# Layer hand-over in a two-layer hybrid backbone: left-over products in two turns, value products between two half norms, early products four pairs at a time, context keys in the weight ring

## Chip, cores and metric

One core of one Trainium2 chip runs the whole program. The metric is device microseconds of one execution, as the median of several. Engines are named as the profile names them: PE (matmul) and PEld (its weight load), DVE, ACT, POOL, and SP, which issues most DMAs. All matmuls here are in the fp32r format, and each logical product is three of them: high by high, high by low and low by high part.

## What is computed

Two layers over 1024 latent tokens of width 1024, with a context of 256 tokens. Layer 0 mixes tokens by retention and by softmax attention, layer 1 by a gated MLP. Each layer ends in a squared-ReLU channel MLP. What bears on the change:

```python
# layer 0, attention: latent queries read context keys and latent keys
s = jnp.einsum('bqkgd,bskd->bkgqs', qi, k) * scale       # k = [context keys 256 | latent keys 1024]
p = jax.nn.softmax(s, axis=-1)
# every layer
x = x + g1 * o_lat
x = x + g2 * (jnp.square(jax.nn.relu(modulate(rms_norm(x, norm2_g), sh2, sc2) @ w1)) @ w2)
# layer 1, mixer
h = modulate(rms_norm(x, norm1_g), sh1, sc1)
z = jax.nn.gelu(h @ w_in); u, v = z[..., :1024], z[..., 1024:]
```

## The kernel before

The stream is held feature-major: eight tiles of 128 features by 1024 tokens, treated as two halves of 512 tokens. A value is split into a high part (an ACT copy that rounds) and a low part (a DVE subtraction); `split` does this (lines 79 to 81). Weights come through a ring of four staging tiles (`st_tile`) and are split into a ring of twelve tiles (`w_tile`, lines 69 to 72). From the end of the attention on, all PSUM tiles come from one pool of eight banks.

**Attention (lines 577 to 654).** `att_load` loads the latent keys `akl` and queries into the weight ring, and the context keys `akc` and values `av` into the pool `ap_`, which opens at line 571 in the place of the pools `hp` and `tabs` (closed at lines 563 and 564). `tabs` holds the cosine and sine tables that `rope` reads (lines 388 to 390). `scores` makes a 128x256 product with `akc` (`s2`) and two 128x512 products with `akl` (`s1`), takes the maximum of both, and writes the exponentials to `pr`; `mx`, `sm` and `pr` are in `ap_` as well.

**Channel MLP.** Both its matrices are multiplied by a scheme of seven block products in place of eight (names A11, A12, S1 to S4, A22 against B11, B21, T1 to T4, B22). Up: sixteen pairs `p` of hidden blocks. For the first eight (`NPRO`), `up_first` (line 847) makes the two products that need the first token half only, A11 by B11 and A12 by B21, two pairs at a time: two B11 blocks, whose results ACT copies to `ef` and SP stores to `e_d`, then two B21 blocks on top in the same bank, squared by ACT into `sf` and stored to `s_d`. Each block is twelve matmuls. After each block `tick()` takes one step of `norm_forms` (line 745) of the second half: the norm's sum (`nsum`), its broadcast (`nbc`) with the first quarter of the forms, then one quarter each; a quarter takes two buffers `t1`, `t2` of the pool tag `t`, which has four buffers and also serves `ef` and `sf`. `mlp_up` (line 782) then takes p = 0 to 15 in order: for p below 8 (`early`) it reads `e_d` and `s_d` back and makes five products, else seven.

Down: `job` (line 884) multiplies a band of hidden blocks; after each product DVE adds the bank to the stream (`stt`, line 882). The last two jobs are called with `keep=True`: the products S1 by T1 (`todo[7]`) and S4 by B22 (`todo[8]`) of output tiles 1 to 3 are handed back as closures, the left-overs. They reach the second token half only. `todo[8]` also holds `done(q, 1)`, which adds the squares of the finished tiles to the norm's sum (`norm_acc`) and stores them with a POOL DMA.

**Hand-over from layer 0 to layer 1 (lines 975 to 1029).** For the first half: `norm_rstd` (four small matmuls `nsum`, DVE, a power on POOL), `norm_bc` (four small matmuls `nbc`), then for each of eight tiles DVE writes `hp`, ACT the high part of `hm` and DVE its low part. Then all left-overs. Then the same norm for the second half. Then the value products `pv` of layer 1: for each of two column groups, eight token tiles `tt` (0 to 3 first half, 4 to 7 second half), each eight steps `k` of three matmuls; the first four tiles of group 0 go step by step side by side. ACT applies GELU to each finished tile (`v_out`).

The order in the program text is not always the order on an engine: within the limits of the data each engine has its own order, which the profile shows.

Of the kernel before, what the change touches and what calls it, by code (L numbers as in the profile page):

```python
# [10 lines left out]
F32 = mybir.dt.float32  # L11
F32R = mybir.dt.float32r
# [4 lines left out]
P = 128  # L17
# [15 lines left out]
def hybrid_retention_gqa_chunkmlp_kernel(tc, I, out):  # L33
# [543 lines left out]
    def att_load(G, hh):  # L577
        if hh == 0:
            akl = load_w(ak_d[G, :, TC:], f"ak{G}")
            akc = ap_.tile([P, 2, TC], F32R, tag="akc", bufs=2, name=f"akc{G}")  # L580
            av = ap_.tile([P, 2, 10 * P], F32R, tag="av", bufs=2, name=f"av{G}")
            avd = av_d[G].rearrange("p n d -> p (n d)")
            for dst, src in ((akc, ak_d[G, :, 0:TC]), (av[:, :, 0:1024], avd[:, 0:1024]), (av[:, :, 1024:], avd[:, 1024:])):
                st = st_tile()[:, :src.shape[-1]]
                nc.sync.dma_start(st, src)
                split(st, dst[:, 0], dst[:, 1])
            kv_t[G] = (akl, akc, av)
        aq_t[2 * G + hh] = load_w(aq_d[2 * G + hh], f"aq{2 * G + hh}")
# [193 lines left out]
    def mlp_up(l, F, s_d, utemp, pro):  # L782
        def src(p):
            return lambda i: [I["w1"][l, p, i]]

        for p in range(16):
            f = w_forms(src(p), f"u{l}_{p}", skip=p in pro)
            a, b, e = (mm_tile([P, H], f"u{n}{l}_{p}") for n in "abe")

# [56 lines left out]

    def up_first(l, F, s_d, e_d):

        for p0 in range(0, NPRO, 2):
            ps = [mm_tile([P, H], f"uf{l}_{p0 + d}") for d in range(2)]  # L850
            W = []
            for d in range(2):
                R = w_raw(I["w1"][l, p0 + d, 0])
                W.append([w_form(R[:, j], f"wf{l}_{p0 + d}_{j}") for j in range(2)])
            for d in range(2):
                block(ps[d], W[d][0], F["B11"], True)
                tick()
                e1 = tmp(f"ef{l}_{p0 + d}")
                nc.scalar.copy(e1, ps[d])
                nc.sync.dma_start(e_d[p0 + d], e1)  # L860
            for d in range(2):
                block(ps[d], W[d][1], F["B21"], False)
                tick()
                s11 = tmp(f"sf{l}_{p0 + d}")
                nc.scalar.activation(s11, ps[d], AF.Relu)
                nc.scalar.activation(s11, s11, AF.Square)
                nc.sync.dma_start(s_d[p0 + d][0], s11)

    def mlp_down(l, xt, s_d, done):
# [14 lines left out]
        def job(*parts, keep=False):  # L884
# [35 lines left out]
            for i in range(7):  # L920
                for go in todo[i]:
                    go()
            return todo[7] + todo[8]

        job((1, 0, 1), (2, 0, 2))
        job((3, 0, 3))
        for i in range(13):
            job((i % 4, i, i + 4))
        left = job((1, 13, 16), keep=True)
        return left + job((2, 14, 16), (3, 15, 16), keep=True)  # L930

    def layer_mlp(l, F, close_xt, s_d, e_d, x1_d, done):
        up_first(l, F, s_d, e_d)
# [40 lines left out]

    close_xd, xt, left = layer_mlp(0, F, close_xa, s_d, e_d, x1_d, done0)
    hm = [[None] * KT for _ in range(2)]
    for hf in range(2):
        if hf:
            for g in left:
                g()  # L980
        rs = norm_rstd(nt, ss1[hf], H)
        pb = norm_bc(rs, H)
        gs, sh = mods[(1, 1)], mods[(1, 0)]
        for k in range(KT):
            hp = tmp("hp")
            hm[hf][k] = o = f_tile(f"hm_{hf}_{k}")
            nc.vector.scalar_tensor_tensor(hp, xt[k][:, hf * H:(hf + 1) * H], gs[:, k:k + 1], pb, ALU.mult, ALU.mult)
            nc.scalar.activation(o[:, 0, :], hp, AF.Identity, bias=sh[:, k:k + 1])
            nc.vector.scalar_tensor_tensor(o[:, 1, :], hp, sh[:, k:k + 1], o[:, 0, :].bitcast(F32),
                                           ALU.add, ALU.subtract)  # L990
    close_xd()


# [3 lines left out]
    nc.sync.dma_start(wsT, I["wsT"])  # L997
    bsb = gp.tile([P, 8, P], F32, name="bsb")
    nc.sync.dma_start(bsb, I["bs"].partition_broadcast(P))
    zg = [f_tile(f"zg{g}", F32).rearrange("p a (b c) -> p (a b) c", c=P) for g in range(8)]  # L1000
    vs = gp.tile([P, 8, NTT], F32, name="vs")
    for cg in range(2):
        W = [load_w(I["wv"][cg, 2 * j:2 * j + 2].rearrange("k p n -> p k n"), f"wv{cg}_{j}") for j in range(4)]
        pvs = {}

        def v_mm(tt, k):
            hf, o = tt // 4, (tt % 4) * P
            if k == 0:
                pvs[tt] = mm_tile([P, H], f"pv{cg}_{tt}")
            wc = slice((k % 2) * H, (k % 2) * H + H)  # L1010
            mm3(pvs[tt], hm[hf][k][:, 0, o:o + P], hm[hf][k][:, 1, o:o + P],
                W[k // 2][0][:, wc], W[k // 2][1][:, wc], k == 0, k == KT - 1)

        def v_out(tt):
            for j in range(4):
                nc.scalar.activation(zg[cg * 4 + j][:, tt, :], pvs[tt][:, j * P:(j + 1) * P], AF.Gelu_apprx_tanh)

        for t0 in (0, 4):
            if cg + t0 == 0:
                for k in range(KT):  # L1020
                    for tt in range(4):
                        v_mm(tt, k)
                for tt in range(4):
                    v_out(tt)
                continue
            for tt in range(t0, t0 + 4):
                for k in range(KT):
                    v_mm(tt, k)
                v_out(tt)
        for j in range(4):  # L1030
            g = cg * 4 + j
            for q in range(2):
# [59 lines left out]
        close_za()  # L1092

    close_xd, xt, left = layer_mlp(1, F, close_xb, s_d, e_d, x1_d, done1)
    for g in left:
        g()
    close_xd()
    close_f()
# [69 lines left out]
```

## Time and profile before

| | us |
|---|---|
| median of 3 runs (lowest, highest) | 2358.17 (2357.75, 2369.09) |
| the profiled execution, whole | 2363.36 |
| its span, first to last instruction | 2361.60 |
| PE busy in the span | 2244.6 (95%) |
| DVE busy | 1645.0 (70%) |
| ACT busy | 1026.2 (43%) |
| POOL busy | 143.3 (6%) |
| mean granted TensorE clock | 0.982 of full |

Busy time is the time in which an engine has at least one instruction under way. A row of the timeline gives the start, the length, the engine, the line of the kernel, the operation with its written and read tiles and shapes, and in brackets how long the engine stood idle before it and what released it. A line can be that of a helper (75 to 77 are the three matmuls of a product, 80 and 81 the two halves of a split), so tiles say more than lines.

### The profile page before, as it was taken

Reading aid. Unit: us, or ns where it says so; the run is one execution under the profiler, and the core shown is the slowest. Engines: PE = TensorE matmul, PEld = TensorE weight load, DVE = VectorE, ACT = ScalarE, POOL = GpSimd, SP = SyncE. Lnnn points to the kernel's source line nnn. Section 1 sums busy time; section 2 is a strip of 40 time slices with the busy share of each in tenths; the row PEclk is TensorE's granted clock in tenths of the full one; section 3 lists DMA queues with packets and bytes.
Section 4 is the critical chain, followed back from the end, with each engine's and each line's share of the span. In section 5 each row is a group of like instructions: output and inputs, shape, how many; then the busy total and the mean of one; then the engine's idle time right before and its main releaser. Section 6 shows DMA issues by size and latency. Waiting matters only on the chain.

```text
span 2361.6 us, 28820 instructions
## 1 busy us (share of the span) xinstructions
PE 2244.6 (95%) x10412; PEld 1807.9 (77%) x10412; DVE 1645.0 (70%) x2706; ACT 1026.2 (43%) x1809; POOL 143.3 (6%) x133
## 2 busy tenths in 40 slices
PE   6998999989999999999999969999999999999999
PEld 1887787769887788877777848888878888777777
DVE  5656679699857786568877673444678755788885
ACT  3511112277736545564444333323465555544441
POOL 2323221000000000000000010000000000000000
PEclk9999999999999999999999979999999999999999
DMA  8244556440153764466445341114447544754442
GB/s 296 74 138 155 159 176 194 138 137 19 36 201 110 232 214 162 147 212 211 150 143 144 98 142 54 45 45 170 138 143 245 170 147 147 276 161 143 147 138 81
DMA packets 158688, 350.71 MB, mean 149 GB/s; under 512 B 16593, under 2 KB 30417, under 8 KB 158545
## 3 DMA queue, kind: packets, MB, share of 16 engines
q1 hardware_dynamic: 154960, 336.28, 44.1%
q0 software_dynamic: 3584, 12.58, 1.4%
q8 instruction: 82, 1.34, 0.2%
q14 instruction: 62, 0.50, 0.1%
HBM read 262.29 MB, written 86.51 MB: 148 GB/s over the span
## 4 chain that ended last, share of the span: by engine, by line
PE 79%; DVE 8%; DMA 6%; issue 3%; ACT 3%; POOL 1%; SPq 0%; DVEq 0%; ACTq 0%; POOLq 0%
PE dbd L75 4%; PE ub L75 4%; PE ub L77 4%; PE ub L76 4%; PE dbd L76 4%; PE dbd L77 4%; PE po L76 3%; PE po L77 3%; PE po L75 2%; PE ue L75 2%; PE ue L76 2%; PE ue L77 2%; PE ded L75 2%; PE pl L77 2%; PE ded L76 2%
## 5 line engine op out<-in xcount | busy, mean ns | idle before, releaser
L80 ACT CAST wr<-st 128x512 fp32r<-128x512 f32 (+2 forms) x404 | 277.8, 693 | 481.9 <-PE dbd L76 90.1
L81 DVE TENSOR_TENSOR wr<-st,wr 128x512 fp32r<-128x512 f32 (+2 forms) x400 | 308.6, 777 | 176.1 <-ACT wr L80 158.0
L75 PE MATMUL dbd<-sT,wr 128*128 128x512 f32 x384 | 155.0, 405 | 13.7 <-DVE xd L882 9.4
L75 PE MATMUL ub<-T,wr 128*128 128x512 f32 x384 | 153.1, 399 | 11.6 <-DVE ur L822 6.8
L75 PE MATMUL pl<-wr,h 128*128 128x512 f32 x384 | 154.5, 402 | 0.2 <-ACT zrl L484 0.2
L76 PE MATMUL dbd<-sT,wr 128*128 128x512 f32 x384 | 153.2, 399 | 0.0
L77 PE MATMUL dbd<-sT,wr 128*128 128x512 f32 x384 | 153.0, 399 | 0.0
L77 PE MATMUL ub<-T,wr 128*128 128x512 f32 x384 | 152.6, 397 | 0.0
L76 PE MATMUL ub<-T,wr 128*128 128x512 f32 x384 | 152.6, 397 | 0.0
L76 PE MATMUL pl<-wr,h 128*128 128x512 f32 x384 | 152.5, 397 | 0.0
L77 PE MATMUL pl<-wr,h 128*128 128x512 f32 x384 | 152.5, 397 | 0.0
L882 DVE SCALAR_TENSOR_TENSOR xd<-dbd,mcol,xd 128x512 f32<-128x512 f32 x152 | 112.9, 747 | 45.7 <-PE dbd L77 45.7
L80 ACT CAST sT<-sT 128x512 fp32r<-128x512 f32 x128 | 79.2, 620 | 83.9 <-DMA sT<-s_d 79.4
L139 DVE SCALAR_TENSOR_TENSOR macc<-st,scc,macc 128x1024 f32<-128x1024 f32 x70 | 92.4, 1321 | 24.2 <-DMA st<-in_mod_w 23.7
L75 PEld LDWEIGHTS dbd<-sT,wr 128*128 128x128 f32 x384 | 73.1, 190 | 39.4 <-DVE xd L882 16.6
L81 DVE TENSOR_TENSOR sT<-sT 128x512 fp32r<-128x512 f32 x128 | 87.3, 686 | 19.0 <-ACT sT L80 18.8
L75 PEld LDWEIGHTS ub<-T,wr 128*128 128x128 f32 x384 | 72.6, 189 | 30.6 <-DVE ur L822 7.7
L81 DVE TENSOR_TENSOR sB<-sB 128x512 fp32r<-128x512 f32 x96 | 66.0, 688 | 33.0 <-ACT sB L80 33.0
L791 ACT ACTIVATE ur<-ur 128x512 f32<-128x512 f32 x96 | 60.8, 633 | 60.6 <-DVE ur L837 22.9
L77 PEld LDWEIGHTS dbd<-sT,wr 128*128 128x128 f32 x384 | 73.0, 190 | 17.7
L80 ACT CAST sB<-sB 128x512 fp32r<-128x512 f32 x96 | 59.5, 620 | 61.4 <-DMA sB<-s_d 59.3
L77 PEld LDWEIGHTS ub<-T,wr 128*128 128x128 f32 x384 | 72.6, 189 | 17.5
(363 smaller groups left out, 5854.0 us busy)
## 6 DMA issues: line engine op xcount, KB each, us to landing
st<-in_w SPq DMA_DIRECT2D x132, 512.0 KB, 4.4
s_d<-ur SPq DMA_DIRECT2D x208, 256.0 KB, 2.3
st<-in_mod_w SPq DMA_DIRECT2D x80, 512.0 KB, 4.4
sT<-s_d SPq DMA_DIRECT2D x128, 256.0 KB, 2.9
sB<-s_d SPq DMA_DIRECT2D x96, 256.0 KB, 3.2
st<-in_wo SPq DMA_DIRECT2D x32, 512.0 KB, 3.6
st<-in_wg SPq DMA_DIRECT2D x24, 512.0 KB, 5.1
mw<-in_mod_w SPq DMA_DIRECT2D x16, 512.0 KB, 6.4
```

The lines of the kernel that those rows point to most:

```text
L75: nc.tensor.matmul(ps, lhsT=a_hi, rhs=b_hi, start=first, stop=False, skip_group_check=more)
L76: nc.tensor.matmul(ps, lhsT=a_hi, rhs=b_lo, start=False, stop=False, skip_group_check=more)
L77: nc.tensor.matmul(ps, lhsT=a_lo, rhs=b_hi, start=False, stop=last, skip_group_check=more)
L80: nc.scalar.copy(hi, src)
L81: eng.tensor_tensor(lo, src, hi.bitcast(F32), ALU.subtract)
L139: nc.vector.scalar_tensor_tensor(acc, st, scc[:, k, 0:1], acc, ALU.mult, ALU.add)
L791: nc.scalar.activation(t, t, AF.Relu)
L882: nc.vector.scalar_tensor_tensor(o, ps_, g, o, ALU.mult, ALU.add)
```

## The change

Four edits. The context keys take a tile of the weight ring in place of one of the pool `ap_`. `up_first` works on four pairs at a time, and `mlp_up` takes pair 8, which needs all seven products, ahead of pairs 0 to 7. The two last down jobs hand their left-overs back as two lists, all S1 by T1 products and all S4 by B22 products. At the hand-over the order becomes: first list, norm and forms of the first half, second list, the value weights of column group 0 and its products for the first token half, norm and forms of the second half, the GELUs of the first four tiles, then the remaining value products.

```diff
     def att_load(G, hh):
         if hh == 0:
             akl = load_w(ak_d[G, :, TC:], f"ak{G}")
-            akc = ap_.tile([P, 2, TC], F32R, tag="akc", bufs=2, name=f"akc{G}")
+            akc = w_tile()[:, :2 * TC].rearrange("p (a b) -> p a b", a=2)
...
-        for p in range(16):
+        for p in [NPRO] + list(range(NPRO)) + list(range(NPRO + 1, 16)):
             f = w_forms(src(p), f"u{l}_{p}", skip=p in pro)
...
-        for p0 in range(0, NPRO, 2):
-            ps = [mm_tile([P, H], f"uf{l}_{p0 + d}") for d in range(2)]
+        for p0 in range(0, NPRO, 4):
+            ps = [mm_tile([P, H], f"uf{l}_{p0 + d}") for d in range(4)]
             W = []
-            for d in range(2):
+            for d in range(4):
                 R = w_raw(I["w1"][l, p0 + d, 0])
                 W.append([w_form(R[:, j], f"wf{l}_{p0 + d}_{j}") for j in range(2)])
-            for d in range(2):
+            for d in range(4):
                 block(ps[d], W[d][0], F["B11"], True)
                 tick()
...
-            for d in range(2):
+            for d in range(4):
                 block(ps[d], W[d][1], F["B21"], False)
                 tick()
...
-            return todo[7] + todo[8]
+            return todo[7], todo[8]
...
-        left = job((1, 13, 16), keep=True)
-        return left + job((2, 14, 16), (3, 15, 16), keep=True)
+        la, lb = zip(job((1, 13, 16), keep=True), job((2, 14, 16), (3, 15, 16), keep=True))
+        return la[0] + la[1], lb[0] + lb[1]
...
-    for hf in range(2):
-        if hf:
-            for g in left:
-                g()
+
+    def norm_rows(hf):
         rs = norm_rstd(nt, ss1[hf], H)
         pb = norm_bc(rs, H)
...
+    def v_weights(cg):
+        for j in range(4):
+            zg[cg * 4 + j] = f_tile(f"zg{cg}{j}", F32).rearrange("p a (b c) -> p (a b) c", c=P)
+        return [load_w(I["wv"][cg, 2 * j:2 * j + 2].rearrange("k p n -> p k n"), f"wv{cg}_{j}") for j in range(4)]
...
+    for g in left[0]:
+        g()
+    norm_rows(0)
+    for g in left[1]:
+        g()
+    wv0 = v_weights(0)
+    for k in range(KT):
+        for tt in range(4):
+            v_mm(0, wv0, tt, k)
+    norm_rows(1)
+    for tt in range(4):
+        v_out(0, tt)
     close_xd()
...
     for cg in range(2):
-        W = [load_w(I["wv"][cg, 2 * j:2 * j + 2].rearrange("k p n -> p k n"), f"wv{cg}_{j}") for j in range(4)]
...
+        W = v_weights(1) if cg else wv0
+        for tt in range(0 if cg else 4, NTT):
+            for k in range(KT):
+                v_mm(cg, W, tt, k)
+            v_out(cg, tt)
...
-    for g in left:
+    for g in left[0] + left[1]:
         g()
```

## Rows read from the trace of the kernel before

**Rows 1.** Page, engines: busy us (share of span) and number of instructions.

```profile
PE 2244.6 (95%) x10412; PEld 1807.9 (77%) x10412; DVE 1645.0 (70%) x2706; ACT 1026.2 (43%) x1809; POOL 143.3 (6%) x133
```

**Rows 2.** Waits of PE, whole run: who waits for whom, total us, times, longest.

```profile
PE nsum L195 <- DVE ss L189: 10.5, 2, 5.3
...
PE ded L75 <- DVE xd L882: 8.2, 8, 4.9
...
PE s L75 <- ACT akc L80: 6.3, 1, 6.3
PE uf L75 <- ACT ef L859: 6.0, 6, 1.2
...
PE ub L75 <- ACT wr L80: 4.8, 2, 2.4
...
PE nbc L205 <- POOL rs L199: 3.9, 3, 1.4
```

**Rows 3.** Timeline of PE at the hand-over: start, length, instruction, idle before it.

```profile
1372.73 0.80 PE L75 MATMUL dbd<-sT,wr 128*128 128x512 f32 x1 [4.06 <-ACT wr L80]
...
1381.54 0.40 PE L77 MATMUL dbd<-sT,wr 128*128 128x512 f32 x1
1387.26 1.87 PE L195 MATMUL nsum<-ones,ss 128*128 128x1 f32 x8 [5.32 <-DVE ss L189]
1390.56 2.08 PE L205 MATMUL nbc<-ident,rs 128*128 128x128 f32 x8 [1.44 <-POOL rs L199]
...
1402.73 0.79 PE L75 MATMUL ded<-sB,w_d 128*128 128x512 f32 x1 [4.92 <-DVE xd L882]
...
1419.97 0.77 PE L75 MATMUL pv<-wr,hm 128*128 128x512 f32 x1
...
1443.00 0.39 PE L75 MATMUL pv<-wr,hm 128*128 128x512 f32 x1
```

**Rows 4.** Timeline of DVE at the hand-over.

```profile
1385.72 1.48 DVE L189 TENSOR_TENSOR ss<-ss,sq 128x512 f32<-128x512 f32 x2
...
1392.68 2.06 DVE L987 SCALAR_TENSOR_TENSOR hp<-xd,mcol,nbc 128x512 f32<-128x512 f32 x3 [3.28 <-PE nbc L205]
1394.66 2.07 DVE L989 SCALAR_TENSOR_TENSOR hm<-hp,mcol,hm 128x512 fp32r<-128x512 f32 x3
```

**Rows 5.** Busy time by stretch: us, PE, PEld, DVE, ACT, POOL, clock, DMA share, GB/s.

```profile
786.00:1056.00 270.00, 266.53 (x1143) 214.47 (x1142) 188.27 (x304) 143.93 (x243) 2.38 (x4) 1.00 0.56 187
1382.00:1420.00 38.00, 19.73 (x69) 16.39 (x69) 24.19 (x37) 10.85 (x18) 6.46 (x10) 0.67 0.28 97
```

**Rows 6.** Timeline of PE in the up stage of layer 0.

```profile
735.15 1.05 PE L195 MATMUL nsum<-ones,ss 128*128 128x1 f32 x8
...
738.94 1.06 PE L205 MATMUL nbc<-ident,rs 128*128 128x128 f32 x8
...
770.09 0.50 PE L75 MATMUL uf<-B,wr 128*128 128x512 f32 x1 [1.16 <-ACT ef L859]
777.12 0.50 PE L75 MATMUL uf<-B,wr 128*128 128x512 f32 x1 [1.16 <-ACT ef L859]
785.35 0.50 PE L75 MATMUL ub<-T,wr 128*128 128x512 f32 x1 [2.38 <-ACT wr L80]
```

**Rows 7.** Instructions on tile uf, 732 to 763 us: ns, first and last start.

```profile
L75 PE MATMUL uf<-B,wr x40: 393/394/482, 732.3 to 761.5; 128*128 128x512 f32 x40
...
L865 ACT ACTIVATE sf<-uf x2: 578/584/591, 747.6 to 755.7; 128x512 f32<-128x512 f32 x2
```

**Rows 8.** Timeline of ACT at the start of the attention.

```profile
478.82 0.41 ACT L80 CAST akc<-st 128x256 fp32r<-128x256 f32 x1 [6.67 <-DVE ropeb L390]
...
482.78 1.28 ACT L606 ACT_TABLE_LOAD   x1
```

**Rows 9.** Timeline of PE at the start of the attention, third query tile.

```profile
485.78 0.50 PE L75 MATMUL s<-wr,wr 128*128 128x512 f32 x1 [2.56 <-ACT pr L607]
```

**Rows 10.** Timeline of ACT, GELUs of the first four token tiles.

```profile
1441.14 2.85 ACT L1016 ACTIVATE zg<-pv 128x128 f32<-128x128 f32 x16 [9.38 <-PE pv L77]
```

More of the change, by code (lines that the diff above doesn't have):

```diff
@@ L990, in hybrid_retention_gqa_chunkmlp_kernel, with v_mm, v_out @@
                                            ALU.add, ALU.subtract)
+    zg = [None] * 8
+    pvs = {}
+    def v_weights(cg):
+        for j in range(4):
+            zg[cg * 4 + j] = f_tile(f"zg{cg}{j}", F32).rearrange("p a (b c) -> p (a b) c", c=P)
+        return [load_w(I["wv"][cg, 2 * j:2 * j + 2].rearrange("k p n -> p k n"), f"wv{cg}_{j}") for j in range(4)]
+    def v_mm(cg, W, tt, k):
+        hf, o = tt // 4, (tt % 4) * P
+        if k == 0:
+            pvs[tt] = mm_tile([P, H], f"pv{cg}_{tt}")
+        wc = slice((k % 2) * H, (k % 2) * H + H)
+        mm3(pvs[tt], hm[hf][k][:, 0, o:o + P], hm[hf][k][:, 1, o:o + P],
+            W[k // 2][0][:, wc], W[k // 2][1][:, wc], k == 0, k == KT - 1)
+    def v_out(cg, tt):
+        for j in range(4):
+            nc.scalar.activation(zg[cg * 4 + j][:, tt, :], pvs[tt][:, j * P:(j + 1) * P], AF.Gelu_apprx_tanh)
+    for g in left[0]:
[10 more added lines that the diff above has]
+        v_out(0, tt)
     close_xd()
@@ L999, in hybrid_retention_gqa_chunkmlp_kernel @@
     nc.sync.dma_start(bsb, I["bs"].partition_broadcast(P))
-    zg = [f_tile(f"zg{g}", F32).rearrange("p a (b c) -> p (a b) c", c=P) for g in range(8)]
     vs = gp.tile([P, 8, NTT], F32, name="vs")
     for cg in range(2):
-        W = [load_w(I["wv"][cg, 2 * j:2 * j + 2].rearrange("k p n -> p k n"), f"wv{cg}_{j}") for j in range(4)]
[L1004 to L1029, printed above, removed]
+        W = v_weights(1) if cg else wv0
[3 more added lines that the diff above has]
+            v_out(cg, tt)
         for j in range(4):
```

## Prediction

> **What bounds the kernel now.** I read the page first: PE is busy for 95% of the span [rows 1], so an edit earns time only where PE stands still. The next view is therefore the table of PE's waits over the whole run [rows 2]. Four kinds of wait in it stand at places that the change touches: the sum of a norm that waits for DVE (10.5 us in two waits), a left-over product `ded` that waits for DVE (8.2), the early products `uf` that wait for ACT's copies `ef` and the first late product `ub` that waits for a weight form (6.0 and 4.8, over two layers), and the first score that waits for the context keys (6.3). The third view, PE's timeline at each of these places, tells what stood ready meanwhile.
>
> At the **hand-over** the last main product of the down stage starts at 1381.54; then PE waits 5.32 us for the sum `ss`, 1.44 us between the norm's sum and its broadcast, and 4.92 us ahead of the second turn of left-overs. The wait for the second sum is the other half of the 10.5 us. The value products start at 1419.97 and those of the second token half at 1443.00 [rows 2, 3]. From 1382 to 1420 PE's clock is granted at 0.67 on average, so the matmuls between the waits run at the lower level (1.2 GHz) for part of the time, and DVE works for 24.19 of the 38 us [rows 5]. So this stretch is a chain of short steps on three engines, with 36 left-over matmuls and 96 value matmuls that lie behind steps they don't depend on.
>
> **Part 1, the hand-over.** The edit moves the first turn of left-overs (18 matmuls) ahead of norm 0, the second turn (18) and the 96 value matmuls of the first token half ahead of norm 1. Nothing is added or removed; every DMA is the same, and the POOL stores of the second turn still precede the power of norm 1. I rebuild the chain:
>
> - A matmul of 512 columns costs 0.245 us at the full clock: 24 of them lie between the starts 770.09 and 777.12, of which 1.16 us is a wait [rows 6]. So a turn of 18 takes 4.4 us. The first runs from about 1381.9 to 1386.3, beside the sums.
> - The sum `ss` of the first half is done at 1387.2, since its two last additions start at 1385.72 and take 1.48 [rows 4]. Nothing in it depends on the left-overs. What could delay it are the three bank additions of the first turn on DVE, which take about the 0.7 us each of the additions beside them: 0 to 2 us; I take 0, because the matmuls that release them end only shortly before the sum.
> - Norm 0: `nsum` 1.05, wait for the power 1.44, `nbc` 1.06 (durations of the same steps when PE was busy before [rows 3, 6]): broadcast done at 1390.8. The first low part of `hm` is done 2.8 us after the end of the broadcast (1392.64 to about 1395.4 [rows 3, 4]): 1393.6.
> - The second turn takes 4.4 us from 1390.8, so PE is the later one, and the value products start at 1395.2 in place of 1419.97. Their forms keep ahead: DVE makes one eighth with two operations of 0.66 us (three in 2.06 [rows 4]), 1.3 us, and PE needs twelve matmuls for it, 2.9 us. The bank additions and squares of the second turn lie beside them.
> - The first half's value products take 23.0 us (1419.97 to 1443.00 [rows 3]): end at 1418.2.
> - The cover is now gone from norm 1: in the kernel before its forms ran beside these 23 us. After the change PE pays `nsum` 1.05, 1.44, `nbc` 1.06 and 2.8 to the first form, 6.35 us. So the second half starts at 1424.6 in place of 1443.00: a gain of 18.4.
> - Behind that, the second half's forms come at 1.3 us per step. If PE goes through one token tile after the other, its first tile ends with the last form, 16 operations of 0.66 or 10.6 us after the broadcast, and 0.7 for the last three matmuls, against 2.8 and 24 matmuls (5.5) without starving: 3.0 us lost. If it fills in the other tiles, nothing is lost. ACT may also put the table load and the 16 GELUs (1.28 and 2.85 [rows 8, 10]) ahead of the forms: up to 4.1 us. The text of the kernel puts the forms first, so I take 1 us for both together.
>
> Part 1 gives 17.4 us. Its bounds are 9.3 (18.4, less 2.0 for bank additions ahead of the sum, 3.0 and 4.1) and 20.0 (the second turn wholly in the power's wait, so that the start is set by the first form at 1393.6).
>
> One rule speaks against this part. The row of the table load shows 1.28 us [rows 8]. By the Trainium skill ("ScalarE: Activation LUTs", What ACT_TABLE_LOAD costs) each switch to another set of functions also costs a drain, 2.66 us in all; then a load ahead of norm 1's forms would cost 1.4 us more, and the sum would be 16.0 in the bad order and unchanged in the good one.
>
> **Part 2, early products and pair 8.** Per layer PE waits about 3 us for `ef` (three waits, two of 1.16) and 2.38 for the first S2 form [rows 2, 6]. The copies are late because of their buffers and their place on ACT, not because of the products: by 763 us PE had done 120 `uf` matmuls, ten blocks, but ACT had squared only two [rows 7]. So the eight B11 blocks were finished, and the B21 blocks stood behind copies that ACT makes after the squares of the pair before. With four pairs in a group, four copies come ahead of four squares, and a B21 block follows its B11 block by three blocks, 8.8 us, in place of one. Pair 8 then gives PE 24 matmuls, 5.9 us, that need only B11 and B21 forms, over a wait of 2.38. All is moved, nothing added; SP's stores and read-backs are the same. The whole of 6.0 + 4.8 = 10.8 us is the upper bound. The lower is 0 or below: four copies hold all four buffers of tag `t` that the second half's `t1` and `t2` need, so a norm step can wait for a store. I take 10.0, since those forms are done long before PE needs them, and a step that comes some us late is covered.
>
> **Part 3, context keys.** PE waits 6.30 us for them, but ACT's copy of them waited for the last reader of the rotary tables [rows 2, 8]. That is the release of the space under the pool `ap_`, and the softmax's own buffers `mx` and `pr` are in the same pool. So the two small score products move forward, but the exponentials stay behind the same release; they also need a table load of 1.28 us, and the third query tile waits for them until 485.78 [rows 8, 9]. What goes is DVE's and ACT's split of the keys and the wait of the maximum for the late product: I take 1 us, with 0 and 2.5 as bounds (2.5 is the wait of the third tile [rows 9]). The keys' two tiles shift the weight ring, so that one output weight less can be made ready before the attention ends; the same 2.5 bounds what that could cost, and I take nothing.
>
> **Sum.** 17.4 + 10.0 + 1.0 = 28.4 us. Against the profiled execution, 2363.36 us (span 2361.60), that is 2335.0; the median of the runs shown is 5.2 us lower, 2358.17, and gives 2329.8.
>
> **Rivals.**
> - *Starved second half.* The wait moves from ahead of the value products to their middle: 3.0 and 4.1 us of Part 1 are paid, 11.3 + 10 + 1 = 22.3, 2336. For it: the forms come at 1.3 us a step and PE's text order is by tile. Against it: the second half's forms stand ahead of the GELUs.
> - *Up stage gains nothing.* The four buffers of tag `t` are the limit, and with four pairs they are held longer: 18.4, 2339.8.
> - *The order on PE stays.* The value products and left-overs were ready during the waits of 5.3 us and PE didn't take them, so the engine's order isn't free: if norm 1 still comes first, the change doesn't do what it says, and only 11 us remain, 2347.
> - *More goes than I count.* The wait of 4.06 us ahead of the last down job [rows 3] goes too, as that job's forms are placed anew: 20.0 + 4.1 + 10.8 + 2.5 = 37.4, 2320.8.
> - *Slower.* Pair 8 first puts seven weight forms in a ring of twelve ahead of the early pairs' five. If each following pair then finds its S2 form late, as the first pair does now, the wait of 2.38 us is paid per pair. It decides from twelve pairs of the 32 on (28.4 / 2.38); with the 16 pairs of one layer it is 38 us, 2368. Against it: from 786 to 1056 PE is busy for 266.5 of 270 us and DVE for 188 [rows 5], so forms are made with room to spare.
>
> **How the numbers follow.** Chances: forecast 0.39, starved second half 0.20, up stage gains nothing 0.12, order stays 0.12, more goes 0.12, slower 0.05. The forecast and three cases on its side hold 0.83, from 2321 to 2340 us; with 9.3 of Part 1 and 3 of Part 2 (one layer's wait for the first form) on the one side, 12.3 us, and the fourth rival with 5 us for other reordering on the other, the range is 2316 to 2346. Half a per cent, 11.8 us, is about what a measurement can tell from no change. Faster by more: 0.83; within: 0.12 (order stays); slower: 0.05.
>
> **What would show it.** PE's timeline after the change: `ded` ahead of the first `nsum`; `pv` from about 1395, less what was gained before it; one wait of 1.4 and one of about 2.8 us around the second `nbc`, in the middle of the value products, and no 5 us wait; no wait of `uf` for `ef` and none of `ub` for a form near 785; a first wait of scores for the keys gone and a wait for `pr` at nearly the same time as before. I am wrong if `pv` still starts behind two norms, if the waits for `ef` stay, or if the waits between `nbc` and the second half of `pv` sum to over 15 us.

## The result and the profile after

| | before | after |
|---|---|---|
| median of the runs beside one another, us | 2358.45 (2357.75 to 2369.09) | 2330.31 (2326.75 to 2337.72) |
| ratio to the kernel before, 95% interval | | 0.9878 (0.9859 to 0.9898) |
| profiled execution, us (span) | 2363.36 (2361.6) | 2337.72 (2335.9) |

The kernel became 1.2% faster: 28.1 us by the medians, 25.6 by the two profiled executions. By stages, in us; the last two columns are means over all kernels of this study in which the stage is as before or as after, with their lowest and highest trace:

| stage | trace before | trace after | all as before | all as after |
|---|---|---|---|---|
| attention: first score to output projection | 170.5 | 171.2 | 170.7 (170.5 to 170.7, six) | 171.1 (170.7 to 171.4, four) |
| up stage, layer 0: first `uf` to first `dbd` | 325.7 | 324.0 | 328.5 (325.7 to 330.4, five) | 323.1 (322.0 to 324.0, four) |
| down stage of layer 0 and value products: first `dbd` to last `pv` | 450.7 | 431.3 | 446.9 (442.6 to 450.7, four) | 429.8 (427.7 to 431.3, five) |
| up stage, layer 1 | 328.2 | 321.8 | 327.5 (326.5 to 328.2, five) | 322.1 (320.8 to 323.5, four) |
| down stage, layer 1 (unchanged) | 325.6 | 324.8 | 323.7 (320.3 to 327.6, all) | |

By the means the hand-over gave 17.1 us, the two up stages 5.4 each, and the attention lost 0.4: 27.5 us of the 28.1. A stage with the same instructions differs by several us from trace to trace, so that a single pair of traces gives 19.4, 1.7 and 6.3 for the same three; the means are the better measure. (One of the five traces behind the 429.8 is that of the kernel without the value weights' low parts, whose hand-over isn't quite that of after.) A narrower stretch spreads less: the last 60 main down products (`dbd` and `dad`), the left-overs, the two norms and the value products, the same 512 matmuls in every kernel. From the first start to the last it takes 149.7 us on the mean of the four kernels with the old hand-over (147.8 to 151.5) and 131.9 on the mean of five with the new one (131.7 to 132.3). By this measure the hand-over gave 17.8 us. PE's idle time in it falls from 23.6 us to 11.1, on the means; for the rest fewer of its matmuls, those of the norms among them, run at the lower clock.

The page and PE's waits over the whole run, as in [rows 1, 2] (who waits for whom: total us, times, longest):

```profile
PE 2243.3 (96%) x10412; PEld 1811.7 (78%) x10412; DVE 1645.4 (70%) x2706; ACT 1023.4 (44%) x1809; POOL 143.3 (6%) x133
```

```profile
PE ub L75 <- DVE ur L822: 8.3, 2, 4.7
PE tal L444 <- ACT av L80: 6.2, 1, 6.2
PE dbd L75 <- DVE xd L882: 6.1, 8, 1.6
...
PE ded L75 <- DVE xd L882: 5.6, 7, 1.5
...
PE nbc L205 <- POOL rs L199: 4.8, 3, 2.3
PE pv L75 <- ACT hm L986: 3.2, 2, 1.6
PE s L75 <- ACT pr L607: 3.1, 2, 2.6
...
PE nsum L195 <- DVE ss L189: 2.7, 1, 2.7
```

PE's busy time over the same instructions is 1.3 us less; the rest of the gain is idle time. Of the four kinds in [rows 2] at places that the change touches, the two for `ef` and for the first S2 form are gone, that for the sum `ss` fell from 10.5 us to 2.7, that of `ded` from 8.2 to 5.6. The wait for the keys has a successor of the same length: `tal`, a transpose, for ACT's copy of the context values.

PE at the hand-over, as in [rows 3] (start, length, instruction, idle before it):

```profile
1363.86 0.39 PE L75 MATMUL ded<-sT,w_d 128*128 128x512 f32 x1
...
1369.54 0.47 PE L75 MATMUL ded<-sB,w_d 128*128 128x512 f32 x1 [1.37 <-DVE xd L882]
...
1385.28 1.05 PE L195 MATMUL nsum<-ones,ss 128*128 128x1 f32 x8 [2.67 <-DVE ss L189]
1388.67 2.08 PE L205 MATMUL nbc<-ident,rs 128*128 128x128 f32 x8 [2.35 <-POOL rs L199]
1392.35 0.79 PE L75 MATMUL pv<-wr,hm 128*128 128x512 f32 x1 [1.59 <-ACT hm L986]
...
1416.44 0.95 PE L195 MATMUL nsum<-ones,ss 128*128 128x1 f32 x8
1418.80 1.16 PE L205 MATMUL nbc<-ident,rs 128*128 128x128 f32 x8 [1.41 <-POOL rs L199]
1421.55 0.80 PE L75 MATMUL pv<-wr,hm 128*128 128x512 f32 x1 [1.59 <-ACT hm L986]
```

Left-over products `ded` now start at 1363.86, among the products of the last down job, and both turns end ahead of the first `nsum`. The job's two waits in the kernel before, of 4.06 us [rows 3] and of 1.71 (at 1366.31), have shrunk to one of 1.37. Behind the job stands one chain (sum, power, broadcast, first high part) and then the value products of the first half, 27.6 us earlier than in [rows 3]; the chain of norm 1 stands in their middle.

Busy time of the same stretch, as in [rows 5], and of two short ones behind waits (us, PE, PEld, DVE, ACT, POOL, clock, DMA share, GB/s):

```profile
1383.00:1421.00 38.00, 29.33 (x128) 24.22 (x128) 21.59 (x33) 8.93 (x15) 4.08 (x5) 0.86 0.20 73
1421.00:1436.00 15.00, 14.45 (x51) 11.67 (x52) 9.74 (x15) 10.13 (x29) 0.00 (x0) 0.79 0.21 71
1053.00:1059.00 6.00, 5.50 (x13) 4.33 (x14) 6.00 (x11) 4.95 (x11) 0.00 (x0) 0.52 0.70 235
```

PE is busy for 29.3 of the 38 us in place of 19.7, and the granted clock is 0.86 in place of 0.67.

### The profile page after: what moved, and what is told of

The parts are those of the page before. It is cut to its first block, busy times and chain, and to the rows that moved or that the text cites. A ratio compares the mean times of both kernels' runs of the same rounds, so it can differ in the third digit from the quotient of the medians.

```text
span 2335.9 us, 28819 instructions
## 1 busy us (share of the span) xinstructions
PE 2243.3 (96%) x10412; PEld 1811.7 (78%) x10412; DVE 1645.4 (70%) x2706; ACT 1023.4 (44%) x1809; POOL 143.3 (6%) x133
## 4 chain that ended last, share of the span: by engine, by line
PE 80%; DVE 8%; DMA 7%; ACT 2%; issue 2%; POOL 1%; SPq 0%; DVEq 0%; ACTq 0%; POOLq 0%
PE ub L77 4%; PE ub L75 4%; PE ub L76 4%; PE dbd L75 4%; PE dbd L76 4%; PE dbd L77 4%; PE po L75 3%; PE po L76 3%; PE po L77 3%; PE ue L75 2%; PE ue L76 2%; PE ue L77 2%; PE pl L77 2%; PE ded L75 2%; PE pl L76 2%; PE pl L75 2%
## 5 line engine op out<-in xcount | busy, mean ns | idle before, releaser
L80 ACT CAST wr<-st 128x512 fp32r<-128x512 f32 (+3 forms) x406 | 278.4, 692 | 490.8 <-PE dbd L76 90.9
L81 DVE TENSOR_TENSOR wr<-st,wr 128x512 fp32r<-128x512 f32 (+3 forms) x402 | 308.4, 774 | 142.7 <-ACT wr L80 124.5
L81 DVE TENSOR_TENSOR sT<-sT 128x512 fp32r<-128x512 f32 x128 | 87.5, 687 | 19.9 <-ACT sT L80 19.7
L75 PEld LDWEIGHTS dbd<-sT,wr 128*128 128x128 f32 x384 | 72.6, 189 | 30.6 <-DVE xd L882 12.7
L75 PEld LDWEIGHTS ub<-T,wr 128*128 128x128 f32 x384 | 73.1, 190 | 27.3 <-DVE ur L822 9.4
L77 PEld LDWEIGHTS ub<-T,wr 128*128 128x128 f32 x384 | 73.2, 191 | 17.5
L76 PEld LDWEIGHTS ub<-T,wr 128*128 128x128 f32 x384 | 73.2, 191 | 17.3
```

Source lines behind the costliest of these rows:

```text
L75: nc.tensor.matmul(ps, lhsT=a_hi, rhs=b_hi, start=first, stop=False, skip_group_check=more)
L76: nc.tensor.matmul(ps, lhsT=a_hi, rhs=b_lo, start=False, stop=False, skip_group_check=more)
L77: nc.tensor.matmul(ps, lhsT=a_lo, rhs=b_hi, start=False, stop=last, skip_group_check=more)
L80: nc.scalar.copy(hi, src)
L81: eng.tensor_tensor(lo, src, hi.bitcast(F32), ALU.subtract)
```

## The experiments

All medians stand beside runs of the kernel before on the same chip; ratios are to it, with the 95% interval. The intervals are 6 to 13 us wide, so where less is at stake the reading goes by waits in the traces.

**Part 1 alone.** The kernel before with the left-overs' two turns and the new order of norms and value products, the rest as before (loops stand on one line here and below, and `...` marks what is left out).

```diff
-        left = job((1, 13, 16), keep=True)
-        return left + job((2, 14, 16), (3, 15, 16), keep=True)
+        la, lb = zip(job((1, 13, 16), keep=True), job((2, 14, 16), (3, 15, 16), keep=True))
+        return la[0] + la[1], lb[0] + lb[1]
...
+    for g in left[0]: g()
+    norm_rows(0)
+    for g in left[1]: g()
+    wv0 = v_weights(0)
...
+    norm_rows(1)
```

> The kernel before with Part 1 alone (left-overs in two turns, first half's value products ahead of norm 1). Theory: Part 1 carries most of the gain by itself and by the same steps as in the whole change: both turns of left-overs run among the last down job's products, the first value product follows the first half's broadcast, the second half starts behind nsum, power, nbc and one high part. Between the start of the down stage and the last value product it should gain 17 to 20 us, and the median should be 2338 to 2342 us (ratio 0.991 to 0.993). Rival A, the parts lean on one another (the early products shift the schedule so that the left-overs find their forms earlier): less than 14 us here, 2345 or more. Rival B, the start of the down stage carried part of it: over 22 us here.

Measured: 2340.12 us against 2359.69, ratio 0.9921 (0.9898 to 0.9944), 19.6 us. From the first `dbd` to the last value product it takes 427.7 us, against 446.9 on the mean (442.6 to 450.7) where the hand-over is as before, and the waits at its hand-over are those of after (2.67, 2.35 and 1.59 us). So Part 1 makes its gain by itself, as the theory has it. 427.7 is 23.0 less than the one trace of before, which touches rival B, but that trace is the longest of its four.

**Part 1 cut in two: left-overs in two turns, norm 1 ahead of the value products.** Against the kernel with Part 1 alone:

```diff
     for g in left[0]: g()
     norm_rows(0)
     for g in left[1]: g()
+    norm_rows(1)
     wv0 = v_weights(0)
     ...
-    norm_rows(1)
```

> Part 1 cut in two: the left-overs in two turns (first turn ahead of norm 0, second between the norms), but norm 1 still ahead of every value product, on the kernel before. Theory: the left-overs' two turns can be placed among the last job's products and fill PE's waits there (5.3 us ahead of nsum and 4.9 us ahead of the second turn in the kernel before); the wait for norm 1's sum and forms stays ahead of the value products or shrinks only by what DVE has less to do. First value product 6 to 10 us earlier, last one the same 6 to 10 us earlier: 2348 to 2352 us. Rival: the value products' place alone makes the gain, and the two turns only change which wait the left-overs fill: under 3 us, 2356 us or more.

Measured: 2352.78 us, ratio 0.9975 (0.9963 to 0.9987), 6.9 us by the medians. The narrower stretch of the hand-over takes 142.5 us against 149.7 on the mean, 7.2 less. PE ahead of norm 1:

```profile
1412.69 1.86 PE L195 MATMUL nsum<-ones,ss 128*128 128x1 f32 x8 [15.14 <-DVE ss L189]
```

With the left-overs gone to the last job nothing is left to do between the norms, and PE waits 15.1 us there. The two turns alone bring some two fifths of Part 1.

**Part 1 cut the other way: value products ahead of norm 1, left-overs in one turn behind norm 0.** Against the kernel with Part 1 alone:

```diff
-    for g in left[0]: g()
     norm_rows(0)
-    for g in left[1]: g()
+    for g in left[0] + left[1]: g()
     ...
     norm_rows(1)
```

> Part 1 cut in two the other way: the left-overs all behind norm 0 as before, the first half's value products ahead of norm 1. Theory: PE still waits about 5 us for the sum of norm 0 unless the engine's order lets left-overs fill it, but norm 1 costs only its 5 us chain in the middle of the value products: 10 to 14 us gained, 2345 to 2348 us. Together with the two-turn kernel this should add up to Part 1's 17 to 20 us. Rival: the scheduler places the left-overs among the last job's products whatever the text order, and this kernel does as well as all of Part 1 (17 us or more); then the two turns are worth nothing.

Measured: 2347.05 us, ratio 0.9956 (0.9930 to 0.9983), 11.8 us by the medians. The narrower stretch takes 139.8 us, 9.9 less than 149.7. PE waits ahead of norm 0 as in [rows 3]:

```profile
1392.85 1.87 PE L195 MATMUL nsum<-ones,ss 128*128 128x1 f32 x8 [5.11 <-DVE ss L189]
```

So the order on PE follows the text as far as it needs to: left-overs written behind norm 0 stay behind it. In the stretch the two halves bring 7.2 and 9.9 us, 17.1 together, and Part 1 whole 17.4 (132.3): the two halves act on different waits. The medians (6.9 and 11.8 for 19.6) agree, but their intervals are too wide to show it alone.

**Part 2 cut in two.** First four early pairs at a time, with the late pairs in their old order:

```diff
-        for p0 in range(0, NPRO, 2):
+        for p0 in range(0, NPRO, 4):
```

> The kernel before with four early pairs at a time and nothing else of the change (the pairs of the up stage in their old order, pair 0 first). Theory: the waits of the early products for ACT's copies go (3.0 us a layer), the wait of the first late product for its S2 form stays (2.4 us a layer), so the up stage of a layer ends 2.5 to 3.5 us earlier; at the turn to the down stage, where PE waits for DVE's addition, up to as much is given back in a layer: 2 to 6 us over the run, 2352 to 2356 us. Rival: the four buffers of tag t hold the early products up whatever the grouping; then nothing is gained and ACT's copies still end the waits, 2358 us.

Then pair 8 first, with the early pairs two at a time:

```diff
-        for p in range(16):
+        for p in [NPRO] + list(range(NPRO)) + list(range(NPRO + 1, 16)):
```

> The kernel before with pair 8 of the up stage first and nothing else of the change (early pairs two at a time). Theory: the first late product finds its forms ready, since pair 8 begins with the two products that need only the first token half: the wait of 2.4 us a layer goes; and where the scheduler puts those products between the early ones, they fill the waits for ACT's copies as well. Up stage of a layer 2.4 to 5.4 us earlier, of which the turn to the down stage gives back up to 3.6: 2350 to 2356 us. Rival, the two edits are additive and separate: the waits for the copies stay at 3.0 us a layer and only 2.4 us a layer go. A second rival, the seven forms of pair 8 put the early pairs' forms late: a new wait of 2 us or more for each early pair, 2370 us or more.

Measured: 2356.39 us, ratio 0.9994 (0.9978 to 1.0011), and 2350.59, ratio 0.9971 (0.9958 to 0.9985). PE's idle time in the up stage, from the first `uf` to 20 us ahead of the first `dbd`, is 5.36 us in each layer of the kernel before, 4.50 with four at a time, 2.08 and 2.40 (layers 0 and 1) with pair 8 first, and 0.71 with both; the four other kernels with that part as before lie within 0.02 us of it. My expectation of the first was wrong. What is left with four pairs at a time are PE's two waits, and ACT's order ahead of the second group's copies shows why the first of them is there:

```profile
770.77 0.50 PE L75 MATMUL uf<-B,wr 128*128 128x512 f32 x1 [2.12 <-ACT ef L859]
784.61 0.50 PE L75 MATMUL ub<-T,wr 128*128 128x512 f32 x1 [2.38 <-ACT wr L80]
```

```profile
767.10 1.15 ACT L866 ACTIVATE sf<-sf 128x512 f32<-128x512 f32 x2
768.15 1.05 ACT L865 ACTIVATE sf<-uf 128x512 f32<-128x512 f32 x2
769.11 1.14 ACT L866 ACTIVATE sf<-sf 128x512 f32<-128x512 f32 x2
770.15 1.06 ACT L859 COPY ef<-uf 128x512 f32<-128x512 f32 x2
772.14 0.59 ACT L859 COPY ef<-uf 128x512 f32<-128x512 f32 x1 [0.93 <-DMA s_d<-sf]
```

The copies of the second group come behind the squares of the first, and these behind casts for the norm's forms: ACT makes no pause from 764.41 until the first copy ends, and there PE's wait ends too. The third copy waits for a store of a square to release a buffer, but PE is at work again by then. The grouping turns three short waits into a longer one. Pair 8 removes all of them, since its first products, which stand among the early ones (`ub` and `ua` from 770.29 on, in after), need neither the copies nor an S2 form. But with pair 8 alone three new waits come up in each layer, 90 to 120 us further on. The wait as in [rows 2], and DVE ahead of the longest of them:

```profile
PE ub L75 <- DVE ur L812: 3.4, 6, 0.9
```

```profile
869.50 0.69 DVE L712 TENSOR_TENSOR s_u<-st 128x512 f32<-128x512 f32 x1 [2.95 <-DMA st<-in_w]
...
873.72 0.68 DVE L812 TENSOR_TENSOR ur<-ub,ur 128x512 f32<-128x512 f32 x1
```

The addition that PE needs stands in DVE's order behind a weight form that waits for its transfer. With both edits these waits are gone; why is not shown. So neither edit does it alone: over both layers the four pairs alone take away 1.7 us of idle time, pair 8 alone 6.2, and both 9.3.

**The context keys alone.**

```diff
-            akc = ap_.tile([P, 2, TC], F32R, tag="akc", bufs=2, name=f"akc{G}")
+            akc = w_tile()[:, :2 * TC].rearrange("p (a b) -> p a b", a=2)
```

> The kernel before with the context keys in the weight ring and nothing else. Theory: the first score products come 6 us earlier, but they only move the wait: the exponentials still wait for the pool of the softmax's buffers, so the third query tile starts within 1.5 us of where it did, the end of the attention within 1 us, and the time is 2357 to 2359 us. Rival: the keys' transfer and split were what delayed the softmax; then the third tile comes 2.5 us earlier and stays so, 2355 us.

Measured: 2359.25 us against 2358.82, ratio 1.0004 (0.9992 to 1.0016). The first exponential starts 13.5 us after the first score product (14.1 before), the attention takes 171.4 us (170.5 before). PE:

```profile
477.37 1.51 PE L444 MATMUL tal<-ident,zal 128*128 128x128 f32 x6 [6.19 <-ACT av L80]
...
482.69 0.79 PE L75 MATMUL s<-wr,wr 128*128 128x512 f32 x1 [2.65 <-ACT pr L607]
```

The wait of 6.3 us for the keys became one of 6.19 us at the same place: ACT has the copies of the context values next in its order, which wait for the rotary tables' last reader, and behind them the copy that PE needs.

**The softmax's buffers in a pool of their own, on the changed kernel** (`pr` and `sm` are moved as `mx` is).

```diff
+    sp_, close_sp = open_pool("sp")
     ap_, close_ap = open_pool("ap")
-        mx = ap_.tile([P, 4], F32, tag="mx", bufs=3, name="mx")
+        mx = sp_.tile([P, 4], F32, tag="mx", bufs=3, name="mx")
```

> The changed kernel with the softmax's buffers mx, sm and pr in a pool of their own, opened ahead of the pool with the context values, so that they lie over space that is released earlier. Theory: the release of that pool's space is what holds the first exponential back; with their own pool the exponentials start some us earlier (the maximum of the first tile follows its scores by about 2 us, near 479 us in place of 484), the third query tile no longer waits, and 2 to 5 us are gained at the start of the attention; the time is 2326 to 2329 us. Rival 1: the maximum and the table load set the time of the first exponential anyway, nothing moves, 2330 us. Rival 2: what the attention gains at its start it gives back at its end, because a head's weights or the context values come no earlier: first score earlier, first output product unchanged.

Measured: 2325.67 us (2325.11 to 2329.04), ratio 0.9860 (0.9840 to 0.9879), the attention 168.1 us. ACT in after and then with the new pool:

```profile
480.57 2.30 ACT L80 CAST av<-st 128x1024 fp32r<-128x1024 f32 x3 [6.65 <-DVE ropeb L390]
...
483.95 1.28 ACT L606 ACT_TABLE_LOAD   x1
485.24 0.47 ACT L606 ACTIVATE pr<-s,mx 128x256 f32<-128x256 f32 x1
```

```profile
469.88 1.28 ACT L607 ACT_TABLE_LOAD   x1
471.93 0.47 ACT L607 ACTIVATE pr<-s,mx 128x256 f32<-128x256 f32 x1 [0.76 <-DVE mx L603]
```

The first exponential starts 4.3 us after the first score product in place of 13.5, and the copy of the values no longer stands ahead of it. 3.1 us of it last to the end of the attention. Against the changed kernel the intervals of the ratios overlap, so the trace carries the reading.

**The same pool, but the keys back in their old place.**

```diff
-            akc = w_tile()[:, :2 * TC].rearrange("p (a b) -> p a b", a=2)
+            akc = ap_.tile([P, 2, TC], F32R, tag="akc", bufs=2, name=f"akc{G}")
```

> The kernel with the softmax's buffers in a pool of their own, but the context keys back in their old pool (the whole change without Part 3, plus the new pool). Theory: both hold the start of the attention, one behind the other: with the old keys the first score waits about 6 us for the copy of the keys, which waits for the rotary tables' last reader, so the new pool's gain is lost again; the first transpose of the probabilities comes 17 to 18 us after the first score product as in the kernel before and in the changed one (13.8 with both), and the attention up to the output projection takes 170 to 171 us (168.1 with both). Time 2329 to 2332 us. Rival: the pool of the softmax was the only limit and Part 3 is worth nothing even now; then the first transpose comes 14 to 15 us after the first score, the attention takes 168 to 169 us, and the time is 2325 to 2327.

Measured: 2331.93 us, ratio 0.9887 (0.9862 to 0.9912). The first exponential comes 14.7 us after the first score, the first transpose 19.1, and the attention takes 173.3 us, over 2 us more than I expected; why it is slower than before is not shown. Keys and pool are two limits, one behind the other: each edit alone gains nothing, and both together 2.5 us against the 170.7 of before (3.1 against the changed kernel).

**A bank of its own for the last product of the up stage, on the changed kernel.**

```diff
+            if p == 15:
+                nc.scalar.copy(e1, b)
+                b = a
-            block(b, f["A22"], F["T4"], False)
+            block(b, f["A22"], F["T4"], p == 15)
-            if early:
+            if early or p == 15:
```

> The changed kernel in which the last pair of the up stage puts its A22 product into a bank of its own (its free bank a, added behind it to a copy of bank b) in place of adding to bank b. Theory: at the turn from the up stage to the down stage PE waits 4.7 us in the first layer and 3.6 in the second for DVE's addition that reads bank b; that addition stands on DVE behind splits of the down stage's operands, which wait for their transfers, so the gain of the early products is lost there. With a bank of its own the last product needs no such wait: the wait goes or falls to under 1.5 us a layer and the time falls by 4 to 8 us, to 2322 to 2326 us. Rival: the down stage's operands come at the same time as before, since their buffers are released by the same products; then PE waits a few us later for a split operand as long as it did for DVE, and the time stays within 1.5 us of 2330.

Measured: 2331.47 us, ratio 0.9883 (0.9861 to 0.9906). The wait for L822 is gone, and the up stage of layer 0 takes 316.7 us in place of 323.1 on the mean. But the stage behind it takes 437.9 in place of 429.8, and PE waits inside it:

```profile
PE dbd L75 <- DVE xd L885: 13.3, 6, 5.4
```

```profile
1063.84 0.69 DVE L81 TENSOR_TENSOR sT<-sT 128x512 fp32r<-128x512 f32 x1 [0.75 <-ACT sT L80]
1064.56 0.69 DVE L81 TENSOR_TENSOR sB<-sB 128x512 fp32r<-128x512 f32 x1
1065.71 0.69 DVE L81 TENSOR_TENSOR sB<-sB 128x512 fp32r<-128x512 f32 x1 [0.45 <-ACT sB L80]
1066.32 0.74 DVE L885 SCALAR_TENSOR_TENSOR xd<-dbd,mcol,xd 128x512 f32<-128x512 f32 x1
```

The wait moved from one DVE instruction to another. In both kernels the addition that PE needs stands in DVE's order behind splits of the down stage's operands `sT` and `sB`, and ahead of these ACT waits for their transfers (in after, 4.14 us at 1049.71). PE's idle time around the turn is 7.4 and 6.0 us in the two layers, against 6.7 and 6.5 in after. Over the traces of all kernels with the old bank it lies between 3.9 and 7.3 us, with no order that goes with an edit. The rival holds: the turn's idle time isn't set by the bank. That the transfers set it is likely (the DMA share is 1.01 in the ten us ahead of PE's wait in after and ahead of the first `dbd` here), but I made no run with fewer of them.

**The value weights without low parts.** DVE's subtractions for them are left out, and the products take the high part twice.

```diff
-        return [load_w(I["wv"][cg, 2 * j:2 * j + 2].rearrange("k p n -> p k n"), f"wv{cg}_{j}") for j in range(4)]
...
+            nc.sync.dma_start(st, I["wv"][cg, 2 * j:2 * j + 2].rearrange("k p n -> p k n"))
+            hi = w_tile()
+            nc.scalar.copy(hi, st)
+            W.append((hi, hi))
```

> The changed kernel without the low parts of the value weights: DVE's subtractions of 128x1024 for them are left out and the products take the high part twice, so that TensorE does the same number of matmuls. Theory: the power on POOL ahead of the first broadcast took 1.94 us in place of 1.01 because DVE ran two of these subtractions, with two inputs from SBUF, beside it; without them it takes 1.0 to 1.1 us and PE's wait ahead of the first broadcast falls from 2.35 to 1.4 us. Rival: the longer power belongs to the place (the first of the two, behind a DVE step of its own) and stays at 1.8 us or more without the subtractions.

One execution, of 2324.46 us, so that only the trace is read. POOL, in after and then without the subtractions:

```profile
1386.69 1.94 POOL L199 TENSOR_TENSOR rs<-ms,mhalf 128x4 f32<-128x4 f32 x1 [1.12 <-DVE ms L197]
1417.74 1.01 POOL L199 TENSOR_TENSOR rs<-ms,mhalf 128x4 f32<-128x4 f32 x1 [29.12 <-DVE ms L197]
```

```profile
1379.51 1.03 POOL L199 TENSOR_TENSOR rs<-ms,mhalf 128x4 f32<-128x4 f32 x1 [1.11 <-DVE ms L197]
```

PE's wait for it falls from 2.35 to 1.44 us. The theory holds to a tenth of a us.

**All three additions together**, with the value weights' load and split ahead of the left-overs (`v_store` makes the output tiles `zg`, which stay in their place).

```diff
+    wv0 = v_weights(0)
     for g in left[0]: g()
     norm_rows(0)
     for g in left[1]: g()
-    wv0 = v_weights(0)
+    v_store(0)
```

> The changed kernel with three more edits: the softmax's own pool, the last up pair's A22 product in a bank of its own, and the value weights loaded and split ahead of the left-overs (their output tiles still behind them). Theory: the pool gives its 3 to 4 us at the start of the attention; the bank moves the wait at the turn to the down stage, where the transfers set the pace (DMA share 0.9 and more there), so PE's idle time at the two turns stays at 6 to 7 us each and nothing is gained; with the value weights ahead, one of the three subtractions leaves the stretch between the sum and the broadcast, the sum comes about 1.5 us earlier behind fewer bank additions, and the first value product 1 to 2.5 us earlier. 2322 to 2326 us. Rival: the turn's gain holds beside the pool, 2316 to 2320. Second rival: the early value weights take the weight ring from the last down job's forms, which wait for it, and the hand-over loses 2 us or more: 2327 to 2330.

Measured: 2324.21 us (2320.49 to 2332.72), ratio 0.9858 (0.9832 to 0.9884). The attention takes 167.7 us; the turn stays (6.9 and 4.8 us idle). The value weights' earlier place gained nothing: from the first `dbd` to the first value product it is 341.7 us, against 340.3 with the bank alone. The power still took 1.94 us, since one subtraction stayed beside it, and five matmuls of the left-overs now stand between the sum and the broadcast.

## Why the prediction was right, and where it wasn't

The time came out as predicted (2330.3 for 2329.8), and the terms nearly so: by the means 17.1 us for Part 1 (17.4 predicted), 10.8 for Part 2 (10.0), -0.4 for Part 3 (1.0). The reasons behind the terms were not all right, and that errors inside each part cancelled this well is in part luck.

**Part 1: right in size and in mechanism, with offsetting steps.** By the two traces, all starts of after less 0.8 us, by which its down stage began later: the value products were to start at 1395.2 and start at 1391.6. The step that failed is the place of the second turn, which I left between the norm's broadcast and the value products. Both turns run in the last job's waits, as in the rival "more goes", so the norm's sum comes 2.7 us earlier than I took (1384.5 for 1387.2), and the first form sets the start, as in the upper bound of the step. Four sizes on the way were off. PE still waits 2.67 us for `ss`, where I took nothing: it is through with the left-overs early, and three of their additions stand among DVE's last steps for the sum. By their starts they take up some 2 us there, which is an estimate:

```profile
1382.61 0.75 DVE L882 SCALAR_TENSOR_TENSOR xd<-ded,mcol,xd 128x512 f32<-128x512 f32 x1
1383.28 0.68 DVE L189 TENSOR_TENSOR ss<-ss,sq 128x512 f32<-128x512 f32 x1
1383.87 0.75 DVE L882 SCALAR_TENSOR_TENSOR xd<-ded,mcol,xd 128x512 f32<-128x512 f32 x1
1384.54 0.69 DVE L189 TENSOR_TENSOR ss<-ss,sq 128x512 f32<-128x512 f32 x1
```

The power took 1.94 us beside the subtractions, and the broadcast behind it 2.08 in place of 1.06, at a granted clock of 0.50. The first value product, on the other hand, came 1.6 us behind the broadcast and not 2.8, at both norms: it needs only the high part of `hm`, for which PE waits by the rows above, and I had counted to the low part. The second half was to start at 1424.6 and starts at 1420.8, so that the 18.4 is 22.2. Behind it 2.8 us are lost where I took 1: not by starving, since PE fills in the other token tiles (no wait between 1421.55 and the last value product), but by 13 matmuls at half the clock. The GELUs came behind the forms, as I took it, so the rival of the starved second half didn't occur. That makes 19.4 by these two traces, of which some 2 us are the long trace of before.

On the table load, the trace shows the order that costs nothing by either price, and no drain beyond the row:

```profile
1430.10 1.28 ACT L1008 ACT_TABLE_LOAD   x1
1431.40 2.83 ACT L1008 ACTIVATE zg<-pv 128x128 f32<-128x128 f32 x16
```

The next activation starts 0.02 us after the load's 1.28. The 2.66 us with a drain that the Trainium skill names ("ScalarE: Activation LUTs", What ACT_TABLE_LOAD costs) is not seen here; the measurement decides.

**Part 2: the size was right, the reason wrong.** I predicted 10.0 us of the 10.8 of waits; 4.6 us of idle time go in each layer, 9.3 in all; the 0.71 us a layer that stay are a new wait for the low part of a form that pair 8's first products need. But I credited the four pairs with 6.0 and pair 8 with 4.8. The split kernels show 0.86 us a layer for the four pairs alone and some 3.1 for pair 8 alone; the rest comes only with both. The step that failed: "a B21 block follows its B11 block by three blocks" holds for the first group, while in the second the copies stand on ACT behind the squares of the first group, and PE waits 2.12 us for the first of them. The rival "up stage gains nothing" was nearly right about the four pairs alone, but not by its reason: that wait ended with ACT's other work, not with the release of a buffer. Pair 8's products fill it, and the four pairs keep away the later waits that pair 8 alone brings. Of the slower rival nothing is seen in after.

The pair of traces alone would have misled here. It shows 1.7 us gained in layer 0, with 3.6 lost at the turn to the down stage: a wait of 4.72 us in place of 3.47, and 12 matmuls behind it that took 5.3 us in place of 2.9 at the lower clock. I read this at first as the gain given back at the turn, and the kernel with the bank of its own was made for it. The kernels in which nothing of the up stage is changed show that the trace of before has the shortest up stage of layer 0 among them, since those 12 matmuls ran at the full clock there.

**Part 3: nothing in place of 1 us.** I had the limit right (the release of the pool, which holds the softmax's buffers too), and the kernel with its own pool shows it. What I counted as still to be gained was taken by the next in ACT's order, the values' copies.

## What to carry to other kernels

When a wait has work behind it that doesn't depend on it, look for the place where that work can be *written* earlier, and then count what the moved work leaves in the other engines' queues: here its additions on DVE held the sum back. Where several things wait for one release, moving one of them gains nothing until the last is moved. And test parts of a change alone where they share a wait, and count the waits of the whole stage then: of the two edits to the up stage either one alone leaves waits that are gone with both, and the trace of the whole couldn't show that.

## What the hardware showed

- **A small step on POOL grew with DVE's work beside it.** The power of 128x4 took 1.01 to 1.03 us with DVE idle and 1.94 with subtractions of 128x1024 running, and 1.03 again when they were left out. The Trainium skill says that POOL shares its SBUF ports with DVE and that a DVE operation with two SBUF inputs locks out a POOL operation that reads SBUF until it ends ("SBUF — State Buffer", SBUF: two separate sides). The trace agrees that POOL waits: the first subtraction ran from 1386.52 to 1387.73, and the power, begun at 1386.69, ended 0.9 us behind it, about as long as it takes alone. By that rule the second subtraction, begun at 1387.65, could have held the power out for longer; it didn't, and it took 1.22 us itself, as it does alone.
- **A wait can cost more than its length.** In after PE stood still for 4.72 us ahead of 1053.50, and the clock was granted at 0.52 from 1053 to 1059, its lower level (1.2 GHz); in the trace of before it stood still for 3.47 us at the same place and the twelve matmuls behind ran at full clock. The length of this wait alone doesn't decide it: waits of 3.38 us (softmax's own pool) and 2.70 us (no low parts) at the same place were followed by a granted clock of 0.50. So two traces of a stage with nearly the same idle time can differ by 2.4 us, and idle time is the better measure of an edit than the stage's duration.
